# A decoder trunk on one NeuronCore: operand blocks transposed by DMA instead of by TensorE

## The chip, the cores and the metric

The kernel runs on one core of one Trainium2 chip. The metric is the device time of one execution in microseconds (us), given as the median of several runs. One more execution was recorded by the hardware profiler, and all rows below come from it.

Engines: TensorE (PE; its weight loads are PEld), VectorE (DVE), ScalarE (ACT), GpSimd (POOL) and SyncE (SP, whose queue issues nearly all DMAs). Each works through its instructions in order and waits for the others by semaphores.

## The reference, cut to what matters

Two layers of a decoder trunk on x of 256 x 1024 float32. The FFN and the norms are left out here but for their calls.

```python
x = x + 0.5 * swiglu(rms_norm(x, ffn1_norm), ffn1_w_gu, ffn1_w_down)
h = rms_norm(x, mix_norm)
u, va, q, k, v, qi, ki, wi, g_a, g_b = split(h @ w_in)   # 512 each for u..qi; 64, 8, 1024, 1024
y_a = (gelu(u) * (tril(w_s) @ layer_norm(gelu(va)) + b_s)) @ w_pa
q, k, qi, ki = rope(q), rope(k), rope(qi), rope(ki)
score = sum_h(relu(qi_h @ ki.T) * wi_h)          # causal; the 64 best keys of each row are kept
y_b = softmax(q @ k.T / 8 over the kept keys) @ v @ w_pb     # 8 heads of 64
x = x + (sigmoid(g_a + b) * y_a + sigmoid(g_b + b) * y_b) @ w_out
x = x + 0.5 * swiglu(rms_norm(x, ffn2_norm), ffn2_w_gu, ffn2_w_down)
```

## The kernel before

The 256 rows are two blocks t = 0, 1 of 128 rows, one row to a partition. Every large product is taken in three passes (`mm3`, L238): both operands are split into a rounded part hi and a remainder lo, and hi x hi, hi x lo and lo x hi are added up in PSUM. The stationary operand has to lie with the contracted dimension on the partitions, so whatever was computed row by row is transposed in 128 x 128 blocks first.

**Weights** come as a list of tiles of 128 x 1024 words (424 columns twice for the gates) in the order of use. `issue_dma` (L101) loads one into one of four raw buffers from the SP queue; `issue_split` (L121) makes hi on ScalarE (L136) and lo on VectorE (L137), in two halves, into one of six buffers of split tiles. `done(n)` (L150) is called when TensorE has used tile n for the last time; it issues the split of the tile six further on, and this issues the load of the tile four beyond that one. On the SP queue the order is that of the program, written out by hand; on the other engines a planner orders the instructions from the program's order and its own estimates of when each is ready.

**A layer** is an FFN, the mixer, and a second FFN. In the FFN each block h of 128 x 256 goes through `h_send` (L300): ScalarE copies the 32-bit words into two planes of 16-bit halves (L303), the SP queue issues one DMA that transposes the planes in 128 x 128 blocks (L305), and `h_join` (L308) puts the halves together again on VectorE (L311) and splits them into hi and lo (L290, L291).

**The mixer** first runs eleven projections (list `PROJ`, L873; loop at L671): the first gate part with ki and wi, then qi (c = 5), k (3), q (2), v (4), va (1), u (0), and four more gate parts. Each is a `proj` (L260) for t = 0 and for t = 1, 24 matmuls each, with four weight tiles. The result is evacuated by `evac` (L638). Work that needs TensorE later is put into `hooks` and runs inside a following `proj`, after its third weight tile (L271). For q, k and qi, `evac` rotates the block on VectorE (`rope`, L433) and hooks `headsT` (L457), which makes four TensorE transposes into a PSUM bank (L460) and one evacuation on ScalarE (L461) into qT, kT or qiT. `index_scores` (L477), hooked in the fourth and fifth projection, multiplies qiT and kiT, takes the relu on ScalarE (L491), adds up the heads on VectorE (L501, L503) and runs eight rounds of MAX8 and MATCH_REPLACE8 (L512, L513). `attn_scores` (L522), hooked in the seventh and ninth, multiplies qT and kT (L530), takes the maxima on VectorE (L543) and the exponentials on ScalarE (L547). `spatial` (L625) leaves the gated values gm in place of u; `operandT` (L603), hooked in the tenth and eleventh projection, transposes them on TensorE (L607) and splits them (`split`, L597). `attn_out` (L553) is spread in steps between the matmuls of the last two projections.

Then come the two output projections (`outproj`, L691), which are multiplied by the gates and merged into gg (`merge`, L710), and the product with w_out (`wout`, L726). For that gg is transposed on TensorE and split by `xT_half` (L225, transposes on L211), two halves for each t; those of t = 1 in `m1` (L740), called in the middle of the second `wout`.

Of the kernel before, what the change touches and what calls it, by code (L numbers as in the profile page):

```python
# [10 lines left out]
F32 = mybir.dt.float32  # L11
F32R = mybir.dt.float32r
I32 = mybir.dt.int32
U16 = mybir.dt.uint16
# [6 lines left out]
P = 128  # L21
# [25 lines left out]
def hybrid_kernel(ctx: ExitStack, tc: tile.TileContext, a: dict, out: bass.AP):  # L47
# [11 lines left out]
    def bank(tag, bufs):  # L59
        return psum.tile([P, 512], F32, name=tag, tag=tag, bufs=bufs)  # L60
# [111 lines left out]
    def rsqrt(dst, v, scale, eng, plus=None):  # L172
# [12 lines left out]
        for i in range(3):  # L185
# [4 lines left out]
            else:  # L190
                eng.tensor_scalar(u, y, y, h, op0=OP.mult, op1=OP.mult)
                eng.tensor_scalar(to, u, 1.5, y, op0=OP.subtract, op1=OP.mult)

    rstd = [None, None]
    xhi, xlo = [None, None], [None, None]
# [12 lines left out]
    def xT_trans(t, h, src, tr=None):  # L208
        tr = tr or bank("tr", 2)
        for i in range(4):  # L210
            PE.transpose(tr[:, i * P:(i + 1) * P], src[:, h * 512 + i * P:h * 512 + (i + 1) * P], ident)  # L211
        return tr
# [11 lines left out]

    def xT_half(t, h, src, gain):  # L225

        tr = xT_trans(t, h, src)
        if gain is None:
            v = tr.rearrange("p (k q) -> p k q", k=4)
            S.copy(xhi[t][:, 4 * h:4 * h + 4, :], v)  # L230
            V.tensor_tensor(xlo[t][:, 4 * h:4 * h + 4, :], v,
                            xhi[t][:, 4 * h:4 * h + 4, :].bitcast(F32), OP.subtract)
            return
        for part in range(2):
            for k in range(4 * h, 4 * h + 4):
                xT_split(t, k, tr, gain, (part,))
# [39 lines left out]
    def ffn_sub(l, f, gain_next, first=None, ahead=None, final=None):  # L276
# [22 lines left out]

        def h_send(h):  # L300

            pl = work.tile([P, 2, 256], U16, name="planes", tag="sc")
            S.copy(pl, h.bitcast(U16).rearrange("p (c b) -> p b c", b=2))  # L303
            plT = work.tile([P, 4, P], U16, name="planesT", tag="wk")
            nc.sync.dma_start_transpose(plT, pl.rearrange("p b c -> p (b c)"))  # L305
            return plT

        def h_join(j, t, plT):  # L308

            w = work.tile([P, 2, P], F32, name="words", tag="rp2")  # L310
            V.tensor_copy(w.bitcast(U16).rearrange("p k (q b) -> p b k q", b=2),  # L311
                          plT.rearrange("p (b k) q -> p b k q", b=2))
            h_split(j, t, w)
# [15 lines left out]
        for j in range(FC):  # L329
            if j == 0 and first is not None:  # L330
                p0, p1 = first()
                h0 = h_evac(j, 0, p0)
                h1 = h_evac(j, 1, p1)
            else:
                if j == FC - 3 and ahead is not None:
                    ahead()
                tiles = take(4)
                h0 = h_evac(j, 0, proj(tiles, 0, 512, False))
                if j < FC - 1:
                    s0 = h_send(h0)  # L340
                h1 = h_evac(j, 1, proj(tiles, 1, 512, True))
            if j == 0:
                if first is not None:
                    s0 = h_send(h0)
                s1 = h_send(h1)
                hooks.append(lambda s0=s0: h_join(0, 0, s0))
                hooks.append(lambda s1=s1: h_join(0, 1, s1))
                continue
            if j < FC - 1:
                s1 = h_send(h1)  # L350
                dt = take(2)
                down(j - 1, 0, dt, False)
                down(j - 1, 1, dt, True)
                h_join(j, 0, s0)
                hooks.append(lambda j=j, s1=s1: h_join(j, 1, s1))
            else:
                h_trans(j, 0, h0)
# [63 lines left out]
    def mixer(l, loads):  # L421
# [34 lines left out]

        def headsT(dst, src, t):  # L457
            tr = bank("tr", 2)
            for i in range(4):
                PE.transpose(tr[:, i * P:(i + 1) * P], src[:, i * P:(i + 1) * P], ident)  # L460
            S.copy(dst[:, :, t * P:(t + 1) * P], tr.rearrange("p (k q) -> p k q", k=4))  # L461

# [139 lines left out]

        def operandT(key, src, t):  # L603
            new_operand(key, t)
            tr = bank("tr", 2)
            for i in range(4):
                PE.transpose(tr[:, i * P:(i + 1) * P], src[:, i * P:(i + 1) * P], ident)  # L607
            split(key, t, tr)

# [12 lines left out]

        gm = [None, None]

# [13 lines left out]
        def evac(kind, c, t, ps, bias):  # L638
# [9 lines left out]
            if c in (2, 3, 5):  # L648
                dst = {2: qT, 3: kT, 5: qiT}[c]
                r = work.tile([P, 512], F32, name="roped", tag="roped", bufs=3)  # L650
                rope(r, ps, t, NH)
                hooks.append(lambda: headsT(dst, r, t))
            elif c == 4:
# [12 lines left out]
            6: [lambda: attn_scores(0)],  # L666
            8: [lambda: attn_scores(1)],
            9: [lambda: operandT("gm", gm[0], 0)],
            10: [lambda: operandT("gm", gm[1], 1)],
        }  # L670
# [51 lines left out]
        xT_half(0, 1, gg[:, 0, :], None)  # L722
        merge(1, 1, True)
        acc = [[bank("dn", 4) for _ in range(2)] for _ in range(2)]

# [14 lines left out]
        def m1():  # L740
            new_xT(1)
            xT_half(1, 0, gg[:, 1, :], None)
            xT_half(1, 1, gg[:, 1, :], None)
        wout(0, 1, range(4), ta, False, mid=m1)
        wout(1, 0, range(4), ta, False)
        wout(1, 1, range(4), ta, True)
# [186 lines left out]
```

## Time and profile before

| | us |
|---|---|
| median of 3 runs | 1102.29 (1101.81 to 1102.33) |
| the profiled execution | 1101.6 |
| its span, first to last instruction | 1099.9 |
| TensorE busy | 1089.0 |
| VectorE busy | 763.4 |
| ScalarE busy | 651.5 |

Busy is the time in which an engine had an instruction under way; register, branch and semaphore instructions and the issue of DMAs don't count. Matmuls are pipelined: the duration of one is longer than the step from one to the next. The profiler's view of who waited for whom takes the idle time in front of an instruction and names what ended it.

### The profile page before, as it was taken

The numbers are of one execution on the slowest core, as the hardware profiler recorded it, in microseconds if no ns is written. First come the engines' busy times: TensorE is split into PE (matmuls) and PEld (weight loads), VectorE is DVE, ScalarE is ACT, GpSimd is POOL, SyncE is SP. The second block draws the span as 40 slices with busy tenths as digits, with TensorE's granted clock in tenths as the row PEclk, the third lists the DMA queues.
The fourth block names the chain that finished last, engine by engine and source line by source line (L and its number), as shares of the span: only waits on it lengthen the run. The fifth ranks groups of instructions, "written<-read, shape, count | busy, mean of one in ns | idle before, by whom it ended". The sixth has DMA issues, their size and how long they took to land.

```text
span 1099.9 us, 15283 instructions
## 1 busy us (share of the span) xinstructions
PE 1089.0 (99%) x5158; PEld 910.3 (83%) x5158; DVE 763.4 (69%) x1568; ACT 651.5 (59%) x1305; POOL 37.3 (3%) x99
## 2 busy tenths in 40 slices
PE   9999999999999999999999999999999999999997
PEld 7788888888988888888888888888889888888885
DVE  7666656889957676666676666678999567666655
ACT  7665556555765665565675565564566547655553
POOL 0000000100000100000010000010000001000001
PEclk9999999999999999999999999999999999999998
DMA  8866675644655575665665666756446464766661
GB/s 296 235 215 202 231 249 168 220 153 134 183 182 166 168 237 187 230 211 194 208 204 181 236 210 218 249 170 211 133 146 205 157 195 141 233 213 211 217 221 66
DMA packets 103358, 216.78 MB, mean 197 GB/s; under 512 B 50544, under 2 KB 51952, under 8 KB 103280
## 3 DMA queue, kind: packets, MB, share of 16 engines
q1 hardware_dynamic: 102848, 215.27, 60.1%
q8 instruction: 40, 0.66, 0.2%
q10 hardware_dynamic: 432, 0.55, 0.2%
q14 instruction: 38, 0.31, 0.1%
HBM read 204.25 MB, written 1.05 MB: 187 GB/s over the span
## 4 chain that ended last, share of the span: by engine, by line
PE 96%; DMA 1%; DVE 1%; ACT 1%; issue 0%; ACTq 0%; SPq 0%
PE acc L240 62%; PE dn L240 29%; PE tr L211 1%; PE dn L581 1%; DMA x<-in_x_dram 1%; PE dn L530 1%; PE dn L486 1%; PE tr L571 0%; PE tr L460 0%; DMA raw<-in_gu_dram 0%; DVE lo L137 0%; DMA xt<-in_xt_dram 0%; PE dn L628 0%; ACT hi L136 0%; ACT junk L200 0%; DVE rs_y L189 0%
## 5 line engine op out<-in xcount | busy, mean ns | idle before, releaser
L137 DVE TENSOR_TENSOR lo<-raw,hi 128x512 fp32r<-128x512 f32 (+1 forms) x768 | 489.1, 677 | 148.8 <-ACT hi L136 147.3
L136 ACT CAST hi<-raw 128x512 fp32r<-128x512 f32 (+1 forms) x768 | 430.1, 611 | 133.5 <-DMA raw<-in_gu_dram 62.1
L240 PE MATMUL acc<-hi,xhi 128*128 128x512 f32 (+1 forms) x1040 | 402.9, 388 | 0.1
L240 PE MATMUL acc<-hi,xlo 128*128 128x512 f32 (+1 forms) x1040 | 400.3, 385 | 0.0
L240 PE MATMUL acc<-lo,xhi 128*128 128x512 f32 (+1 forms) x1040 | 399.8, 385 | 0.0
L240 PEld LDWEIGHTS acc<-hi,xhi 128*128 128x128 f32 x1040 | 195.2, 188 | 37.8 <-issue 1.3
L240 PEld LDWEIGHTS acc<-hi,xlo 128*128 128x128 f32 x1040 | 195.3, 188 | 35.8 <-issue 0.7
L240 PEld LDWEIGHTS acc<-lo,xhi 128*128 128x128 f32 x1040 | 195.4, 188 | 35.7 <-DVE lo L137 0.6
L240 PE MATMUL dn<-hi,hh 128*128 128x512 f32 x348 | 136.8, 393 | 0.3 <-ACT hh L290 0.3
L240 PE MATMUL dn<-hi,hl 128*128 128x512 f32 x348 | 135.6, 390 | 0.0
L240 PE MATMUL dn<-lo,hh 128*128 128x512 f32 x348 | 135.5, 389 | 0.0
L290 ACT CAST hh<-words 128x256 fp32r<-128x256 f32 x80 | 32.4, 406 | 97.5 <-DVE words L311 97.5
L282 ACT ACTIVATE sg<-acc,rstd 128x256 f32<-128x256 f32 x86 | 40.7, 473 | 66.6 <-PE acc L240 66.4
L240 PEld LDWEIGHTS dn<-hi,hh 128*128 128x128 f32 x348 | 65.4, 188 | 13.8 <-ACT hh L290 0.7
L240 PEld LDWEIGHTS dn<-hi,hl 128*128 128x128 f32 x348 | 65.3, 188 | 13.8
L240 PEld LDWEIGHTS dn<-lo,hh 128*128 128x128 f32 x348 | 65.4, 188 | 13.1
L311 DVE COPY words<-planesT 128x512 uint16<-128x512 uint16 x80 | 36.7, 460 | 53.5 <-DMA planesT<-planes 53.5
L284 DVE SCALAR_TENSOR_TENSOR h<-acc,rstd,sg 128x256 f32<-128x256 f32 x86 | 41.4, 481 | 39.2 <-ACT sg L282 38.8
L303 ACT COPY planes<-h 128x512 uint16<-128x512 uint16 x80 | 49.3, 618 | 20.7 <-DVE h L284 19.9
L291 DVE TENSOR_TENSOR hl<-words,hh 128x256 fp32r<-128x256 f32 x80 | 33.7, 422 | 17.2 <-ACT hh L290 17.0
L200 ACT ACTIVATE junk<-x 128x1024 bf16<-128x1024 f32 x13 | 13.8, 1058 | 26.4 <-DVE x L400 21.3
L220 ACT ACTIVATE xhi<-tr,gains 128x128 fp32r<-128x128 f32 x80 | 22.3, 376 | 6.5 <-PE tr L211 6.5
(145 smaller groups left out, 719.9 us busy)
## 6 DMA issues: line engine op xcount, KB each, us to landing
raw<-in_gu_dram SPq DMA_DIRECT2D x175, 512.0 KB, 4.5
raw<-in_dn_dram SPq DMA_DIRECT2D x88, 512.0 KB, 6.0
raw<-in_win_dram SPq DMA_DIRECT2D x48, 512.0 KB, 4.2
raw<-in_wg_dram SPq DMA_DIRECT2D x40, 424.0 KB, 3.9
raw<-in_wo_dram SPq DMA_DIRECT2D x16, 512.0 KB, 4.4
raw<-in_pa_dram SPq DMA_DIRECT2D x8, 512.0 KB, 5.3
raw<-in_pb_dram SPq DMA_DIRECT2D x8, 512.0 KB, 3.9
bias<-in_bg_dram SPq DMA_DIRECT2D x10, 212.0 KB, 5.4
```

What stands on the lines that cost most here:

```text
L136: S.copy(hi[:, c], r[:, c])
L137: V.tensor_tensor(lo[:, c], r[:, c], hi[:, c].bitcast(F32), OP.subtract)
L200: S.activation(junk, X[t], AF.Square, accum_out=ss)
L211: PE.transpose(tr[:, i * P:(i + 1) * P], src[:, h * 512 + i * P:h * 512 + (i + 1) * P], ident)
L220: S.activation(xhi[t][:, k, :], v, AF.Copy, scale=g)
L240: PE.matmul(dst, a1, b1, start=start and n == 0, stop=stop and n == 2)
L282: S.activation(sg, ps[:, :256], AF.Silu, scale=rstd[t])
L284: V.scalar_tensor_tensor(h, ps[:, 256:], rstd[t], sg, op0=OP.mult, op1=OP.mult)
L290: S.copy(hh, v)
L291: V.tensor_tensor(hl, v, hh.bitcast(F32), OP.subtract)
L303: S.copy(pl, h.bitcast(U16).rearrange("p (c b) -> p b c", b=2))
L311: V.tensor_copy(w.bitcast(U16).rearrange("p k (q b) -> p b k q", b=2), plT.rearrange("p (b k) q -> p b k q", b=2))
```

## The change

`h_send` becomes three helpers: `planes` (ScalarE copies the words into two planes of half words), `turn` (the DMA transpose from the SP queue) and `join` (the halves into words again, on an engine that is given). The FFN calls them with the sizes, tags and engines as before. New users are, in each layer: the rotated q, k and qi of both t (`planes` right behind `rope`; `turn` in the hook that held the TensorE transposes; `join` on ScalarE one hook later, straight into qT, kT or qiT); the gated values of both t (`gm_send`, hooked in the ninth and tenth projection, and `gm_join` one projection later); and the second half of the merged gates of t = 1 (`turn` right behind the last `merge`, `join` in a new `m2` in the middle of the third `wout`). Each of these is 128 x 512 words, so 128 x 1024 half words. The other three halves of gg, all of x, and ki are transposed on TensorE as before.

```diff
--- before.py
+++ after.py
@@ -191,6 +191,24 @@
                 eng.tensor_scalar(u, y, y, h, op0=OP.mult, op1=OP.mult)
                 eng.tensor_scalar(to, u, 1.5, y, op0=OP.subtract, op1=OP.mult)
 
+
+    def planes(src, tag):
+
+        pl = work.tile([P, 2, src.shape[-1]], U16, name="planes", tag=tag)
+        S.copy(pl, src.bitcast(U16).rearrange("p (c b) -> p b c", b=2))
+        return pl
+
+    def turn(pl, tag, bufs=None):
+        k = pl.shape[-1] // P
+        plT = work.tile([P, 2, k, P], U16, name="planesT", tag=tag, bufs=bufs)
+        nc.sync.dma_start_transpose(plT.rearrange("p b k q -> p (b k) q"), pl.rearrange("p b c -> p (b c)"))
+        return plT
+
+    def join(dst, plT, eng):
+
+        (S.copy if eng is S else eng.tensor_copy)(
+            dst.bitcast(U16).rearrange("p k (q b) -> p b k q", b=2), plT)
+
     rstd = [None, None]
     xhi, xlo = [None, None], [None, None]
 
@@ -222,9 +240,9 @@
             V.scalar_tensor_tensor(xlo[t][:, k, :], v, g, xhi[t][:, k, :].bitcast(F32),
                                    op0=OP.mult, op1=OP.subtract)
 
-    def xT_half(t, h, src, gain):
-
-        tr = xT_trans(t, h, src)
+    def xT_half(t, h, src, gain, turned=False):
+
+        tr = src if turned else xT_trans(t, h, src)
         if gain is None:
             v = tr.rearrange("p (k q) -> p k q", k=4)
             S.copy(xhi[t][:, 4 * h:4 * h + 4, :], v)
@@ -297,19 +315,9 @@
                 PE.transpose(tr[:, i * P:(i + 1) * P], h[:, i * P:(i + 1) * P], ident)
             h_split(j, t, tr[:, :256].rearrange("p (k q) -> p k q", k=2))
 
-        def h_send(h):
-
-            pl = work.tile([P, 2, 256], U16, name="planes", tag="sc")
-            S.copy(pl, h.bitcast(U16).rearrange("p (c b) -> p b c", b=2))
-            plT = work.tile([P, 4, P], U16, name="planesT", tag="wk")
-            nc.sync.dma_start_transpose(plT, pl.rearrange("p b c -> p (b c)"))
-            return plT
-
         def h_join(j, t, plT):
-
             w = work.tile([P, 2, P], F32, name="words", tag="rp2")
-            V.tensor_copy(w.bitcast(U16).rearrange("p k (q b) -> p b k q", b=2),
-                          plT.rearrange("p (b k) q -> p b k q", b=2))
+            join(w, plT, V)
             h_split(j, t, w)
 
         def down(j, t, tiles, last):
@@ -337,17 +345,17 @@
                 tiles = take(4)
                 h0 = h_evac(j, 0, proj(tiles, 0, 512, False))
                 if j < FC - 1:
-                    s0 = h_send(h0)
+                    s0 = turn(planes(h0, "sc"), "wk")
                 h1 = h_evac(j, 1, proj(tiles, 1, 512, True))
             if j == 0:
                 if first is not None:
-                    s0 = h_send(h0)
-                s1 = h_send(h1)
+                    s0 = turn(planes(h0, "sc"), "wk")
+                s1 = turn(planes(h1, "sc"), "wk")
                 hooks.append(lambda s0=s0: h_join(0, 0, s0))
                 hooks.append(lambda s1=s1: h_join(0, 1, s1))
                 continue
             if j < FC - 1:
-                s1 = h_send(h1)
+                s1 = turn(planes(h1, "sc"), "wk")
                 dt = take(2)
                 down(j - 1, 0, dt, False)
                 down(j - 1, 1, dt, True)
@@ -454,11 +462,9 @@
                 V.tensor_tensor(dst, t1[:, None, :w].to_broadcast([P, copies, w]),
                                 t2[:, None, :w].to_broadcast([P, copies, w]), OP.add)
 
-        def headsT(dst, src, t):
-            tr = bank("tr", 2)
-            for i in range(4):
-                PE.transpose(tr[:, i * P:(i + 1) * P], src[:, i * P:(i + 1) * P], ident)
-            S.copy(dst[:, :, t * P:(t + 1) * P], tr.rearrange("p (k q) -> p k q", k=4))
+        def headsT(dst, pl, t):
+            plT = turn(pl, "plT")
+            hooks.append(lambda: join(dst[:, :, t * P:(t + 1) * P], plT, S))
 
         def kiTrans(src, t):
             tr = bank("tr", 2)
@@ -600,12 +606,14 @@
             S.copy(dhi, v)
             V.tensor_tensor(dlo, v, dhi.bitcast(F32), OP.subtract)
 
-        def operandT(key, src, t):
-            new_operand(key, t)
-            tr = bank("tr", 2)
-            for i in range(4):
-                PE.transpose(tr[:, i * P:(i + 1) * P], src[:, i * P:(i + 1) * P], ident)
-            split(key, t, tr)
+        def gm_send(t):
+            gmT[t] = turn(planes(gm[t], "ge"), "plT")
+
+        def gm_join(t):
+            new_operand("gm", t)
+            w = work.tile([P, 4, P], F32, name="words", tag="rp2")
+            join(w, gmT[t], S)
+            split("gm", t, w.rearrange("p k q -> p (k q)"))
 
         def layer_norm(t, ge):
             st = small.tile([P, 6], F32, name="bst", tag="bst")
@@ -620,7 +628,7 @@
                 vn[0], vn[1] = both[:, 0, :], both[:, 1, :]
             V.scalar_tensor_tensor(vn[t], ge, r, lnb, op0=OP.mult, op1=OP.add)
 
-        gm = [None, None]
+        gm, gmT = [None, None], [None, None]
 
         def spatial(t):
             ps = bank("dn", 4)
@@ -649,7 +657,8 @@
                 dst = {2: qT, 3: kT, 5: qiT}[c]
                 r = work.tile([P, 512], F32, name="roped", tag="roped", bufs=3)
                 rope(r, ps, t, NH)
-                hooks.append(lambda: headsT(dst, r, t))
+                pl = planes(r, "ge")
+                hooks.append(lambda: headsT(dst, pl, t))
             elif c == 4:
                 S.activation(vv[:, t, :], ps, AF.Copy, scale=rstd[t])
             elif c == 0:
@@ -664,9 +673,9 @@
             3: [lambda: index_scores(0)],
             4: [lambda: index_scores(1)],
             6: [lambda: attn_scores(0)],
-            8: [lambda: attn_scores(1)],
-            9: [lambda: operandT("gm", gm[0], 0)],
-            10: [lambda: operandT("gm", gm[1], 1)],
+            8: [lambda: attn_scores(1), lambda: gm_send(0)],
+            9: [lambda: gm_join(0), lambda: gm_send(1)],
+            10: [lambda: gm_join(1)],
         }
         for i, (kind, c) in enumerate(PROJ):
             hooks.extend(after.get(i, []))
@@ -721,6 +730,7 @@
         xT_half(0, 0, gg[:, 0, :], None)
         xT_half(0, 1, gg[:, 0, :], None)
         merge(1, 1, True)
+        g1T = turn(planes(gg[:, 1, 512:1024], "ge"), "b2", 4)
         acc = [[bank("dn", 4) for _ in range(2)] for _ in range(2)]
 
         def wout(t, n2, ks, tiles, rel, mid=None):
@@ -740,9 +750,13 @@
         def m1():
             new_xT(1)
             xT_half(1, 0, gg[:, 1, :], None)
-            xT_half(1, 1, gg[:, 1, :], None)
+
+        def m2():
+            w = work.tile([P, 4, P], F32, name="words", tag="b2", bufs=4)
+            join(w, g1T, S)
+            xT_half(1, 1, w.rearrange("p k q -> p (k q)"), None, True)
         wout(0, 1, range(4), ta, False, mid=m1)
-        wout(1, 0, range(4), ta, False)
+        wout(1, 0, range(4), ta, False, mid=m2)
         wout(1, 1, range(4), ta, True)
         tb = take(4)
         wout(0, 0, range(4, 8), tb, False)
```

## Rows read from the trace of the kernel before

**Rows 1.** The page: busy us by engine; the chain that ended last.

```profile
PE 1089.0 (99%) x5158; PEld 910.3 (83%) x5158; DVE 763.4 (69%) x1568; ACT 651.5 (59%) x1305; POOL 37.3 (3%) x99
...
PE 96%; DMA 1%; DVE 1%; ACT 1%; issue 0%; ACTq 0%; SPq 0%
```

**Rows 2.** TensorE's waits, last of three: waiting line, releaser: us, times, longest.

```profile
PE dn L240 <- ACT hh L290: 0.3, 1, 0.3
```

**Rows 3.** Groups by line and shape, TensorE: busy us, mean ns, idle before.

```profile
L460 PE MATMUL tr<-ident,roped 128*128 128x128 f32 x48 | 7.2, 271 | 0.0
...
L211 PE MATMUL tr<-ident,gg 128*128 128x128 f32 x32 | 4.1, 272 | 0.0
...
L607 PE MATMUL tr<-ident,uu 128*128 128x128 f32 x16 | 2.5, 280 | 0.0
```

**Rows 4.** Timeline of TensorE around one group: start us, duration us, instruction.

```profile
208.84 0.39 PE L240 MATMUL acc<-hi,xlo 128*128 128x512 f32 x1
209.07 0.60 PE L460 MATMUL tr<-ident,roped 128*128 128x128 f32 x4
...
209.74 0.40 PE L240 MATMUL acc<-lo,xhi 128*128 128x512 f32 x1
```

**Rows 5.** Groups by line and shape, ScalarE.

```profile
L303 ACT COPY planes<-h 128x512 uint16<-128x512 uint16 x80 | 49.3, 618 | 20.7 <-DVE h L284 19.9 <-DMA fgain<-in_fgain_dram 0.6 <-DVE lo L137 0.3
...
L200 ACT ACTIVATE junk<-x 128x1024 bf16<-128x1024 f32 x13 | 13.8, 1058 | 26.4 <-DVE x L400 21.3 <-DVE x L823 4.5
...
L461 ACT COPY qT<-tr 128x512 f32<-128x512 f32 x4 | 2.3, 585 | 6.8 <-PE tr L460 6.8
```

**Rows 6.** Line 305, the DMA transposes: duration ns min/median/max on the queue; landing.

```profile
L305 SPq DMA_TRANSPOSE planesT<-planes x80: 1189/1197/2396, 25.6 to 1068.5; - x80
...
DMA to landing us min/median/max: 2.3/2.3/7.4
```

**Rows 7.** Waits of the SP queue.

```profile
SPq L112 <- DVE lo L137: 346.8, 202, 10.1
```

**Rows 8.** Stretches: length, then busy PE, PEld, DVE, ACT, POOL; clock, DMA share, GB/s.

```profile
232.00:243.00 11.00, 11.00 (x60) 8.84 (x59) 10.81 (x33) 6.49 (x13) 0.68 (x1) 1.00 0.35 111
243.00:265.00 22.00, 22.00 (x105) 18.04 (x105) 21.36 (x67) 13.39 (x23) 1.67 (x3) 1.00 0.48 148
```

**Rows 9.** Timeline of VectorE; in brackets, idle time before and what ended it.

```profile
229.20 0.29 DVE L501 TENSOR_SCALAR sc<-rr,wi 128x128 f32<-128x128 f32 x1 [2.48 <-ACT rr L491]
...
243.25 0.35 DVE L501 TENSOR_SCALAR sc<-rr,wi 128x256 f32<-128x256 f32 x1
...
270.70 0.69 DVE L543 TENSOR_REDUCE mx<-satt 128x4 f32<-128x512 f32 x1
...
275.09 1.11 DVE L137 TENSOR_TENSOR lo<-raw,hi 128x424 fp32r<-128x424 f32 x2
```

**Rows 10.** Timeline of ScalarE.

```profile
228.57 1.09 ACT L491 ACTIVATE rr<-dn 128x512 f32<-128x512 f32 x2 [0.50 <-PE dn L486]
...
271.42 0.40 ACT L547 ACTIVATE pr<-satt,mx 128x128 f32<-128x128 f32 x1 [2.21 <-DVE mx L543]
...
274.52 1.87 ACT L136 CAST hi<-raw 128x424 fp32r<-128x424 f32 x4
```

**Rows 11.** Timeline of TensorE at the third weight tile of the eighth projection.

```profile
275.68 0.35 PE L240 MATMUL acc<-hi,xhi 128*128 128x424 f32 x1
275.87 0.36 PE L240 MATMUL acc<-lo,xhi 128*128 128x424 f32 x1
```

**Rows 12.** Timeline of the SP queue, three places.

```profile
223.49 0.33 SPq L112 DMA_DIRECT2D raw<-in_win_dram  x1
...
241.44 0.33 SPq L112 DMA_DIRECT2D raw<-in_win_dram  x1
...
348.33 1.53 SPq L112 DMA_DIRECT2D raw<-in_gu_dram  x2
```

**Rows 13.** Timeline of ScalarE in the product with w_out.

```profile
354.25 4.27 ACT L136 CAST hi<-raw 128x512 fp32r<-128x512 f32 x8 [4.17 <-PE dn L240]
```

## The prediction

> **What bounds the kernel now.** I read the page first: TensorE is busy for 99% of the span, and 96% of the chain that ended last is TensorE work [rows 1]. A busy TensorE can still stand and wait, so next comes the view of who waited for whom, on TensorE: it has three rows, two of them from the kernel's first 7 us, and the last is 0.3 us [rows 2]. So TensorE practically never waits, and an instruction taken from its stream is worth its own time, as long as the other engines still deliver in time when TensorE comes earlier. That condition is the question here, so the other views look at the stage where the change lies, the projections of the mixer: how full VectorE is there, and how late each operand is.
>
> **What is removed from TensorE.** The groups by shape give 48 transposes on L460, 16 on L607 and 32 on L211 of gg [rows 3]. The first two disappear, and of the last a quarter (t = 1, second half): 48 + 16 + 8 = 72 transposes in 18 groups of four, nine groups per layer. Their mean of 272 ns is a latency, not what the stream pays. The timeline shows that [rows 4]: from the last matmul before a group to the second one after it 209.74 - 208.84 = 0.90 us pass, where two plain steps take 2 x 0.227 = 0.45 (208.84 to 209.07 is one). A group costs 0.45 us: four steps of about 0.09 to 0.11 and a slow first matmul behind it. 18 x 0.45 = 8.0 us on the path, 4.0 per layer (2.7 by the six groups of qi, k and q, 0.9 by gm, 0.4 by gg). This is the ceiling.
>
> **What is added, by engine.** *ScalarE:* `planes` on 512 words is a copy of 1024 half words; the 512-element one takes 0.618 us and a 1024-element activation 1.058 [rows 5], so about 1.05. `join` in the other direction is likewise 1.05 (it writes with a stride of two where the known copy reads with one; between 0.6 and 2.1 as bounds, I take 1.05, the row of the same size). The twelve evacuations of L461 at 0.585 go [rows 5]. Twelve times (2.1 - 0.6) plus six times 2.1 is 31 us on an engine that is busy 652 of 1100 us [rows 1]; it is free work only where nothing stands behind it. *Sync queue:* 18 more transposes, each twice as wide as the 80 that exist. Those hold the queue for 1.2 us and land 2.3 us after issue, at worst 7.4 [rows 6]. Twice the blocks: between 1.2 and 2.4 on the queue and between 2.3 and 4.6 to landing; I take 2.4 and 3.5 (the wait for the last byte is not doubled). Behind a transpose on this queue stand the weight loads. The loads themselves mostly wait there for VectorE to free a raw buffer, 346.8 us in 202 waits [rows 7], so a transpose largely fills time in which the queue stands anyway; I cost that at nothing, and where the cover is gone the next weight tile comes up to 2.4 us late. *VectorE:* no instruction is added; its subtractions for gm and gg read SBUF in place of PSUM, with as many elements, which I cost at nothing. The renamed FFN helpers issue what they issued before.
>
> **Where the time may be lost again.** While topk runs, VectorE is busy 10.81 of 11 and 21.36 of 22 us [rows 8]. Its saturated stretch begins at 229.20, when the relu of the first index scores releases it, and runs almost without a hole to the maxima of the first attention scores, the first of which starts at 270.70 and ends at 271.39 [rows 9]. ScalarE, in order, stands for 2.21 us before the exponentials until that maximum is there, does eight of them, and only then, at 274.52, the conversion of the third weight tile of the next projection [rows 10]; VectorE's subtraction of it follows at 275.09, two halves in 1.11 [rows 9], so the first half is ready at about 275.65. TensorE begins that tile at 275.68 and needs the subtracted half one step later, at 275.87 [rows 11]. The slack is 0.2 us. TensorE will come to this place 2.7 us earlier, VectorE only by the amount A by which its stretch ends earlier, so TensorE stalls 2.7 - 0.2 - A = 2.5 - A in each layer.
>
> A is at most what TensorE has gained when it does the first index scores: four groups (qi twice, k twice) x 0.45 = 1.8. The relu of these scores, now at 228.57 [rows 10], is ready at 226.8. But `join` of k's first block is due on ScalarE just then: its transpose stands behind the load at 223.49 [rows 12], which is some 1.0 earlier then, issues at about 222.8, lands at 226.2 and is joined until 227.3. That holds the relu back by 0.5, and A = 1.3. The stall is 2.5 - 1.3 = 1.2 per layer, 2.4 in all. Bounds: 0.7 per layer with A = 1.8, and no bound but the transposes' lateness on the other side (rivals).
>
> At the end of the mixer the transpose of the merged gates stands behind the two loads that begin at 348.33 and end at 349.86 [rows 12]. It lands at 353.4, and join and split of that half (1.05 + 0.6) hold ScalarE until 355.05; the conversions of the next weight tiles began at 354.25 [rows 13], so they come 0.8 later. I cost that at 0.2 per layer: the bounds are 0, if TensorE is as far from needing them as that, and 0.8, if it waits for them already, and no wait of that stage stands among TensorE's [rows 2]. gm's joins have a whole projection between sending and use: nothing, and if a probability tile's copy stands behind one, up to 1.
>
> Sum: 8.0 - 2.4 - 0.4 = 5.2 us gained. The profiled execution took 1101.6 us (span 1099.9); it becomes 1096.4. The median of the runs is 0.7 above that execution, so 1102.29 - 5.2 = 1097.1.
>
> **A rule that speaks against the change.** In the trace four transposes of TensorE cost 0.45 us of its stream [rows 4], and a DMA transpose of four blocks lands 2.3 us after issue [rows 6], outside that stream. The Trainium skill (VectorE: DVE Perf Modes, The three transpose paths, with its Rules for kernel authors) says to transpose 128 x 128 on TensorE when a PSUM destination will do, and gives 1309 ns for one block by DMA. As an estimate by that page, eight blocks take 10.5 us; the row's 2.3 us for four contradicts so long a time, and the measurement decides. What late transposes would do here is the fourth rival.
>
> **The rivals.**
> 1. *The full gain.* If the conversion of that third weight tile is put ahead of the exponentials in ScalarE's order, the tie is gone: 8.0 - 0.2 gives 1094.5. For it: TensorE frees that tile's buffer 2.7 us earlier, before the exponentials can start. Against: the order in the trace has it behind them although ScalarE stood idle for 2.21 us [rows 10]. Chance 0.22.
> 2. *ScalarE too full.* If planes and joins make conversions 1 to 1.5 us late inside VectorE's full stretch, VectorE stands in front of them and A falls to 0: stall 2.5 per layer, 8.0 - 5.0 - 0.4 = 2.6, giving 1099.7. For it: VectorE has no room there to wait in [rows 8]. Against: in its first 11 us ScalarE has 6.49 us of work [rows 8]; one planes and two joins for two evacuations make it 6.49 + 3.15 - 1.17 = 8.5, and that fits. Chance 0.17.
> 3. *Slower: join of q in front of the second relus.* The transpose of q's first block stands behind the load at 241.44, which waits for VectorE [rows 7, 12]. Shifted by 1.3 it issues at 240.5 and lands at 244.0 to 245.1. If its join is ordered in front of the four relus of the second index scores, these come at 245.0 to 246.2, and VectorE, which used the first at 243.25 [rows 9], wants it at 241.95 and stands until 245.6 to 246.8, some 3.6 to 4.9. Then A = -2.3 to -3.6, the stall is 4.8 to 6.1 per layer, and 8.0 - 9.6 - 0.4 = -2.0 to -4.6: 1104.3 to 1106.9. It loses from A below -1.5 (stall over 4.0). Against: the relus need TensorE alone, which is early, and the join needs a late load. Chance 0.10.
> 4. *Transposes as late as the worst row*, 7.4 us to landing [rows 6]: q's join then holds ScalarE until about 249, the conversions behind it are some 3 us late, A = -1.5, and the gain is 8.0 - 8.0 - 0.4: 1102.7. Chance 0.05.
>
> **How the numbers follow.** The forecast (stall 0.7 to 2 per layer, 1095.5 to 1098.9) has 0.46. What a measurement can tell from no change is 0.2%, 2.2 us: the line for faster is 1100.1. Faster takes the forecast, the full gain and half of rival 2: 0.46 + 0.22 + 0.08 = 0.76. Within 0.2% (1100.1 to 1104.5) lie the other half of rival 2, rival 4 and the mild end of rival 3: 0.15. Slower gets the rest of rival 3: 0.09. The range reaches from the ceiling, 1102.3 - 8.0 less a little, 1093.8, to 1102.8, which leaves out rival 3 and some 0.04 below.
>
> **What would show it.** TensorE has 5086 instead of 5158 matmuls and no tr rows of roped and uu; the Sync queue has 98 transposes, the new ones at about 2.4 us. ScalarE has 18 copies planes and 18 words or head copies of about 1.05. TensorE's waits show a new row on the weights (hi or lo, L136/L137) of 1 to 1.5 us near the first gate projection behind the attention scores, in both layers. Were there no such row, rival 1 is right; were it over 4 us, with VectorE's relu wait (sc on rr) long, rival 3. The forecast is wrong as a whole if a stall appears in the FFN stages, which the change leaves alone, or if a group turns out cheaper than 0.45.

## The result and the profile after

| | us |
|---|---|
| before, median of 6 runs on the same chip | 1102.07 (1101.24 to 1104.13) |
| after, median of 6 runs | 1108.97 (1108.07 to 1109.76) |
| ratio after to before | 1.0059, 95% interval 1.0049 to 1.0070 |
| profiled execution of after, and its span | 1109.76, 1108.0 |

The change costs 6.9 us; the prediction said 5.2 us gained, with a range that ended at 1102.8. The profiled execution is the slowest of the six. Five lines of the page and of TensorE's waits show the kind of failure: the busy times by engine, the chain that ended last, and who kept TensorE waiting (waiting line, releaser: us in all, times, longest).

```profile
PE 1088.4 (98%) x5086; PEld 905.9 (82%) x5086; DVE 761.9 (69%) x1568; ACT 680.0 (61%) x1329; POOL 37.5 (3%) x99
...
PE 78%; issue 11%; DVE 5%; DMA 3%; ACT 3%; POOL 0%; SPq 0%; ACTq 0%; POOLq 0%
...
PE dn L587 <- ACT pT L579: 3.1, 3, 2.3
...
PE acc L258 <- DVE rs_y L183: 1.3, 2, 0.7
PE acc L258 <- ACT vv L663: 1.3, 1, 1.3
```

The 72 transposes are gone (5086 matmuls in place of 5158 [rows 1]) and ScalarE has 28.5 us more, near the 31 that were foreseen. But the chain is no longer TensorE alone: its share fell from 96% [rows 1] to 78%, and TensorE now waits for ScalarE and VectorE within the mixer, which it never did before [rows 2].

Where this happens can be read off TensorE's position. The table gives, for some weight tiles (counted from 0 in the order of use), how much later than in the trace of before TensorE starts on the tile. The projections of layer 1 use the tiles 66 to 109 (four each), those of layer 2 the tiles 258 to 301. The first row is what each execution lost before the mixer, where the renamed helpers do the same work as before: 0.2 and 0.9 with the whole change in it, 2.1 with the least, so it is not put down to the change.

| tile | what comes there | after | gated values back on TensorE (e1) | transposes left out (e3) | both repairs (e7) |
|---|---|---|---|---|---|
| 66 | layer 1, first projection | 0.9 | 1.1 | 2.1 | 0.2 |
| 85 | heads transposed | -1.9 | -1.7 | -0.7 | -2.7 |
| 93 | end of VectorE's full stretch | 0.2 | 0.2 | -0.6 | -2.5 |
| 103 | before the gated values' joins | 0.2 | 0.2 | -0.6 | -2.3 |
| 106 | behind the first of them | 3.5 | 0.2 | -1.0 | -2.7 |
| 130 | layer 1, mixer done | 3.0 | -0.3 | -1.9 | -3.6 |
| 277 | layer 2, heads transposed | 0.1 | -3.1 | -4.7 | -6.4 |
| 285 | end of VectorE's full stretch | 3.1 | -0.7 | -4.5 | -6.2 |
| 302 | behind the gated values | 8.5 | -0.7 | -5.4 | -7.0 |
| 383 | last tile | 8.0 | -1.1 | -5.8 | -7.5 |

In after each layer gains 2.8 us while the heads leave TensorE, as reckoned (2.7), and loses it again at two places: 2.1 and 3.0 us inside VectorE's full stretch, and 3.3 and 5.4 us at the gated values (net of what the groups gain that leave there). The FFN stages add nothing (3.0 at tile 130 and at 258).

**The gated values.** Timeline of ScalarE in after, layer 1, with the idle time in front of an instruction and what ended it in brackets; then the SP queue.

```profile
292.01 1.36 ACT L209 COPY words<-planesT 128x1024 uint16<-128x1024 uint16 x1 [4.38 <-DMA planesT<-planes]
293.38 1.28 ACT L553 ACT_TABLE_LOAD   x1
294.68 0.51 ACT L553 ACTIVATE pr<-satt,mx 128x256 f32<-128x256 f32 x1
...
298.63 1.87 ACT L136 CAST hi<-raw 128x424 fp32r<-128x424 f32 x4
...
308.46 1.36 ACT L209 COPY words<-planesT 128x1024 uint16<-128x1024 uint16 x1 [3.77 <-DMA planesT<-planes]
```

```profile
280.17 5.62 SPq L112 DMA_DIRECT2D raw<-in_wg_dram  x4
286.54 0.33 SPq L169 DMA_DIRECT2D bias<-in_bg_dram  x1
286.92 1.51 SPq L204 DMA_TRANSPOSE planesT<-planes  x1
...
302.70 1.23 SPq L204 DMA_TRANSPOSE planesT<-planes  x1
```

The planes were ready at 281.3 and 282.8, but the turns stand behind four weight loads and a bias load in the queue's written order, or a whole projection later, and go out at 286.92 and 302.70. ScalarE's order has the join in front of the table load, the eight exponentials and four weight conversions; ScalarE stands for 4.38 us with all of them behind it. TensorE's own waits there are 0.73 and 0.58 us in layer 1 (at 299.21 and 300.25) and 0.39, 0.58, 0.46 and 2.31 us in layer 2 (844.26 to 860.70); in each layer the granted clock falls behind them, which takes some 1.7 us more (an estimate, worked out in the last section). Together that is 3.0 of the 3.3 us and all of the 5.4.

**The heads.** Timeline of ScalarE around both sets of relus in after.

```profile
226.75 1.35 ACT L209 COPY kT<-planesT 128x1024 uint16<-128x1024 uint16 x1 [1.49 <-DMA planesT<-planes]
227.96 1.04 ACT L198 COPY planes<-roped 128x1024 uint16<-128x1024 uint16 x1
228.90 1.09 ACT L497 ACTIVATE rr<-dn 128x512 f32<-128x512 f32 x2
...
240.60 1.37 ACT L209 COPY qT<-planesT 128x1024 uint16<-128x1024 uint16 x1 [2.36 <-DMA planesT<-planes]
241.83 1.04 ACT L198 COPY planes<-roped 128x1024 uint16<-128x1024 uint16 x1
242.76 2.06 ACT L497 ACTIVATE rr<-dn 128x512 f32<-128x512 f32 x4
```

In front of each set of relus stand a join, its wait and a copy into planes. With 0.9 for the start taken off, the first relus come 0.6 earlier than before (228.57 [rows 10]), not 1.8, and the second ones at 241.86, no earlier than before (241.67). The second relus and the second maximum (`mx`) of before:

```profile
241.67 2.07 ACT L491 ACTIVATE rr<-dn 128x512 f32<-128x512 f32 x4 [0.47 <-PE dn L486]
```

```profile
271.36 0.69 DVE L543 TENSOR_REDUCE mx<-satt 128x4 f32<-128x512 f32 x1
```

VectorE's scores wait for the relus in after (the last lines are the maxima of layer 1 and the first of layer 2):

```profile
229.54 0.29 DVE L507 TENSOR_SCALAR sc<-rr,wi 128x128 f32<-128x128 f32 x1 [1.10 <-ACT rr L497]
243.39 0.35 DVE L507 TENSOR_SCALAR sc<-rr,wi 128x256 f32<-128x256 f32 x1 [0.58 <-ACT rr L497]
270.86 0.68 DVE L549 TENSOR_REDUCE mx<-satt 128x4 f32<-128x512 f32 x1
...
272.25 0.68 DVE L549 TENSOR_REDUCE mx<-satt 128x4 f32<-128x512 f32 x1
...
816.26 0.68 DVE L549 TENSOR_REDUCE mx<-satt 128x4 f32<-128x512 f32 x1
```

In layer 2 half of the loss stands at another wait. Of the 3.0 us, 1.5 are lost between the tiles 277 and 278, where TensorE stands 1.34 us at 793.56 (the row vv above). It needs the PSUM bank that ScalarE frees when it evacuates the values v of t = 0, and ScalarE comes to that only behind the join of the queries' second half:

```profile
791.62 1.34 ACT L209 COPY qT<-planesT 128x1024 uint16<-128x1024 uint16 x1 [1.40 <-DMA planesT<-planes]
792.83 0.68 ACT L663 ACTIVATE vv<-acc,rstd 128x512 f32<-128x512 f32 x1
```

In e1 below this wait is 0.25 us and layer 2 still loses 2.4 there, so VectorE's stretch would have taken most of the 1.5 anyway; that is argued from the two traces.

### The profile page after: what moved, and what is told of

Its sections match the earlier page's. It is cut to its first block, busy times and chain, and to the rows that moved or that the text cites. A ratio compares the mean times of both kernels' runs of the same rounds, so it can differ in the third digit from the quotient of the medians.

```text
span 1108.0 us, 15207 instructions
## 1 busy us (share of the span) xinstructions
PE 1088.4 (98%) x5086; PEld 905.9 (82%) x5086; DVE 761.9 (69%) x1568; ACT 680.0 (61%) x1329; POOL 37.5 (3%) x99
## 3 DMA queue, kind: packets, MB, share of 16 engines
HBM read 204.25 MB, written 1.05 MB: 185 GB/s over the span
## 4 chain that ended last, share of the span: by engine, by line
PE 78%; issue 11%; DVE 5%; DMA 3%; ACT 3%; POOL 0%; SPq 0%; ACTq 0%; POOLq 0%
PE acc L258 46%; PE dn L258 29%; DVE lo L137 2%; DMA planesT<-planes 2%; PE dn L802 1%; ACT hi L136 1%; DMA bias<-in_bg_dram 1%; PE tr L229 1%; ACT pr L553 1%; DVE wk L519 1%; DVE m L518 1%; PE dn L587 0%; DMA xt<-in_xt_dram 0%; POOL wk L514 0%; PE dn L536 0%
```

## The experiments

All ratios are to the kernel before in runs on the same chip (its medians there: 1102.48, 1102.41 and 1102.47).

**e1, the gated values back on TensorE.** The heads and the quarter of the merged gates stay on the DMA.

```diff
-            8: [lambda: attn_scores(1), lambda: gm_send(0)],
-            9: [lambda: gm_join(0), lambda: gm_send(1)],
-            10: [lambda: gm_join(1)],
+            8: [lambda: attn_scores(1)],
+            9: [lambda: operandT("gm", gm[0], 0)],
+            10: [lambda: operandT("gm", gm[1], 1)],
```

> The changed kernel with the gated values (gm) transposed on TensorE again; heads and merged gates by DMA. Theory A (ScalarE stands in order in front of a join whose transpose lands 5 to 7 us after issue, with the exponentials and weight conversions behind it): in the trace TensorE loses 3.3 us at gm's joins in layer 1 and 5.4 in layer 2, net of what its two fewer groups give. Without them 1109.0 - 8.7 = 1100.3. Theory B (it is the added ScalarE work that costs, wherever it lies): gm is 4 of 18 joins, so 4/18 of the loss of 6.9 + 8.0 = 14.9 goes, 3.3, and 1.8 of TensorE's gain with it: about 1107.5. Theory C (weight loads are late behind the transposes on the Sync queue): as B, by the number of transposes.

Measured 1100.99, ratio 0.9986 (0.9976 to 0.9995). The gated values account for 8.0 us (1108.97 less 1100.99; 8.4 with each taken against before on its own chip); the place where they lose is the right one, and theories B and C are some 6.5 us off. The heads' loss stays (table).

**e2, only the gated values by DMA.** The other half: `headsT` and the merged gates as before.

> Only gm by DMA; heads and merged gates on TensorE as before. Theory A: before plus 8.7, 1110.8, with ScalarE idle in front of each gm join for 3 to 5 us. Theory B and C: 1102.1 - 1.8 + 3.3 = 1103.6.

Measured 1112.29, ratio 1.0085 (1.0067 to 1.0102). Alone this part costs 9.8 us, 1.1 more than was foreseen. ScalarE stands 18.7 us in front of the four joins, up to 6.5 at a time.

**e3, the ceiling.** The 72 transposes are left out and nothing takes their place: the blocks go on unturned.

```diff
-            tr = bank("tr", 2)
-            for i in range(4):
-                PE.transpose(tr[:, i * P:(i + 1) * P], src[:, i * P:(i + 1) * P], ident)
-            S.copy(dst[:, :, t * P:(t + 1) * P], tr.rearrange("p (k q) -> p k q", k=4))
+            S.copy(dst[:, :, t * P:(t + 1) * P], src.rearrange("p (k q) -> p k q", k=4))
```

> The 72 TensorE transposes are left out, and nothing is put in their place: the blocks are copied or split untransposed, so this part of the computation is missing. It measures the term 18 groups x 0.45 us. If the groups cost what the prediction says and nothing else binds: 1102.1 - 8.0 = 1094.1. If the prediction's tie to VectorE's full stretch holds as well (A = 1.8, stall 0.7 per layer): 1095.5, with waits of TensorE on hi or lo near the eighth projection. If a group costs only its 128-column share, 0.25 us: 1097.6.

Measured 1094.97, ratio 0.9933 (0.9918 to 0.9948): 7.5 us, and 7.9 between the traces (-5.8 at the last tile less 2.1 at the start). The 0.45 us a group [rows 4] are confirmed. TensorE waits nowhere in the mixer, so the tie that the prediction saw in VectorE's stretch costs nothing when no join stands in front of the relus.

**e4, all joins on GpSimd.**

```diff
-            hooks.append(lambda: join(dst[:, :, t * P:(t + 1) * P], plT, S))
+            hooks.append(lambda: join(dst[:, :, t * P:(t + 1) * P], plT, G))
-            join(w, gmT[t], S)
+            join(w, gmT[t], G)
-            join(w, g1T, S)
+            join(w, g1T, G)
```

> All 18 new joins on GpSimd in place of ScalarE; planes stay on ScalarE, transposes as in the change. Theory A: GpSimd waits for the landings instead, with nothing urgent behind it: ScalarE's waits on planesT vanish, and the time falls to 1095 to 1098 (the stall at VectorE's full stretch stays). Theory B: the same direction, 24 of 43 us of added ScalarE work gone: 1109.0 - 0.57 x 14.9 = 1100.5. Theory C: transposes and loads stand as they did, 1109.

Measured 1100.96, ratio 0.9987 (0.9978 to 0.9997). That is theory B's figure and not theory A's 1095 to 1098; what parts the two is e5, with the same work. ScalarE waits for no turn any more and the loss at the gated values is gone, but 3 us per layer are still lost in VectorE's stretch (-2.2 at tile 85, 0.8 at 93). The reason is probably another one. GpSimd, then VectorE, in this kernel:

```profile
240.04 1.61 POOL L209 COPY qT<-planesT 128x1024 uint16<-128x1024 uint16 x1 [4.33 <-DMA planesT<-planes]
243.65 1.69 POOL L209 COPY qT<-planesT 128x1024 uint16<-128x1024 uint16 x1 [2.00 <-DMA planesT<-planes]
```

```profile
240.56 1.58 DVE L137 TENSOR_TENSOR lo<-raw,hi 128x512 fp32r<-128x512 f32 x1
242.33 0.68 DVE L137 TENSOR_TENSOR lo<-raw,hi 128x512 fp32r<-128x512 f32 x1
...
243.65 0.47 DVE L509 SCALAR_TENSOR_TENSOR sc<-rr,wi,sc 128x256 f32<-128x256 f32 x1
244.24 1.31 DVE L509 SCALAR_TENSOR_TENSOR sc<-rr,wi,sc 128x256 f32<-128x256 f32 x1
```

Under each of these two joins one VectorE instruction takes 0.84 or 0.90 us longer than its like (1.31 for 0.47, 1.58 for 0.68), 1.7 us in a stretch that has no room. Under the two joins of the keys, at 227.91 and 230.82, two more take 0.55 and 0.67 longer. Together that is 3.0 us, the size of the loss in layer 1; that it is the cause is argued from these sizes. The Trainium skill (SBUF — State Buffer, SBUF: two separate sides) calls the port pair of the two engines an exclusive lock: of a VectorE operation with two SBUF inputs and a GpSimd one that reads SBUF, the one that starts first blocks the other to its end. The rows above agree: both lengthened instructions end just behind the join (242.14 behind 241.65, 245.55 behind 245.34).

**e5, the gated values' turns sent early.** The same work on every engine; `gm_send` runs behind the loads of the tiles 104 and 105.

```diff
             if last:
                 done(n)
+                if sends and len(sends) > q:
+                    sends[q]()
...
+            sends = [lambda: gm_send(0), lambda: gm_send(1)] if i == 7 else None
-            evac(kind, c, 1, proj(tiles, 1, w, True), bias)
+            evac(kind, c, 1, proj(tiles, 1, w, True, sends=sends), bias)
```

> Same work as in the changed kernel on every engine; only the two turns of the gated values are issued earlier on SP's queue, right behind the loads of the tiles 104 and 105 (about 281.3 and 283.3 us in layer 1, where the planes are ready at 281.3 and 282.8) and no longer at 286.9 and 302.7. Theory A (ScalarE stands in front of a transfer that was sent late, with the exponentials and the weight conversions behind it): with landings of 4.5 to 5.5 us the planes are back by 289, before the exponentials are due at 290; the losses of 3.3 and 5.4 us go, and 1108.97 - 8.7 = 1100.3, or from the run without gm's part 1101.0 - 4 x 0.45 = 1099.2. Theory B (ScalarE has too much work there: 4 x (1.04 + 1.36) = 9.6 us of planes and joins in both layers): the work is the same, so no less than 1107.

Measured 1099.32, ratio 0.9969 (0.9958 to 0.9981), as theory A has it (1099.2 to 1100.3). At the gated values it is not the work on ScalarE, it is the wait. ScalarE in e5:

```profile
285.45 1.36 ACT L209 COPY words<-planesT 128x1024 uint16<-128x1024 uint16 x1 [1.53 <-DMA planesT<-planes]
286.68 1.87 ACT L136 CAST hi<-raw 128x424 fp32r<-128x424 f32 x4
288.46 1.35 ACT L209 COPY words<-planesT 128x1024 uint16<-128x1024 uint16 x1
...
291.20 0.51 ACT L555 ACTIVATE pr<-satt,mx 128x256 f32<-128x256 f32 x1
```

The exponentials begin 3.5 us sooner than in after (291.20 for 294.68; 0.3 of that is the start), although the first turn needs 5.1 us to land here too.

**e6, joins behind the relus.** e1, and in addition the joins of the keys' and queries' first half wait for the relus, by a copy of one word of a relu's result (`relu[0]`) that the join overwrites. The scores' hooks (`index_scores`, `attn_scores`) are put ahead of the other hooks; that part isn't in the lines below.

```diff
+            def late_join():
+                if t == 0 and dst is not qiT:
+                    S.copy(dst[:1, 0, :1], relu[0][:1, :1])
+                join(dst[:, :, t * P:(t + 1) * P], plT, S)
-            hooks.append(lambda: join(dst[:, :, t * P:(t + 1) * P], plT, S))
+            hooks.append(late_join)
```

> Gated values transposed on TensorE as before the change (as in e1_no_gm, 1101.0). Heads by DMA, but the joins of the keys' and queries' first half stand behind the relus of the index scores on ScalarE instead of ahead of them; all else the same. Theory A (the loss of 2.1 to 2.9 us per layer between the tiles 85 and 93 is VectorE's full stretch starting late, because each relu stands behind a join of 1.36 us and the wait in front of it): the relus start some 1.4 us earlier against TensorE's position (about 227.6 and 241.0 in layer 1), and 1.3 to 1.9 us per layer come back: 1097.2 to 1098.4. Theory C (weights arrive late because their loads stand behind the turns on SP's queue) or D (planes and joins as such make ScalarE late with the weight conversions): neither is touched, 1100.5 to 1101.5.

Measured 1096.88, ratio 0.9947 (0.9932 to 0.9962): 4.1 us less than e1 (1100.99) and 0.3 below the hopeful end of theory A. ScalarE in e6:

```profile
226.77 1.05 ACT L198 COPY planes<-roped 128x1024 uint16<-128x1024 uint16 x1 [1.45 <-DVE roped L460]
227.72 1.08 ACT L502 ACTIVATE rr<-dn 128x512 f32<-128x512 f32 x2
...
238.93 1.04 ACT L198 COPY planes<-roped 128x1024 uint16<-128x1024 uint16 x1 [1.88 <-DVE roped L460]
239.88 2.06 ACT L502 ACTIVATE rr<-dn 128x512 f32<-128x512 f32 x4
```

The weight loads stand behind the same turns as in e1 and ScalarE has the same copies, so neither of these (theories C and D) was the cause. The order of the hooks and the wait of the joins were changed together, here and in e7 and e8; no run parts them.

**e7, both repairs.** The whole change with the edits of e5 and e6.

> The two edits above together, nothing of the change undone: gated values' turns early, joins of the keys' and queries' first half behind the relus. Theory A for both: 1099.7 (the mean of 1099.2 and 1100.3) less 2.6 to 3.8 = 1096 to 1097. If only the early turns count: 1099.2 to 1100.3. If neither: 1107 or more.

Measured 1094.58, ratio 0.9929 (0.9912 to 0.9945). It lies 1.4 us below what theory A gave for both. It beats both kernels, before by 7.8 us and after by 14.4 (after was timed on another chip), and gets what e3 gets without any transposing. TensorE waits 2.6 us at the kernel's start and 0.7 after it, and the chain reads as that of before did:

```profile
PE 96%; DMA 1%; DVE 1%; ACT 1%; issue 0%; SPq 0%; ACTq 0%
```

The first and the second maximum of layer 1 in e7:

```profile
268.12 0.68 DVE L557 TENSOR_REDUCE mx<-satt 128x4 f32<-128x512 f32 x1
...
269.51 0.68 DVE L557 TENSOR_REDUCE mx<-satt 128x4 f32<-128x512 f32 x1
```

**e8, which relus decide.** e7 with the queries' join in front of the second relus again (`if t == 0 and dst is kT`).

> As e7_both (1094.6), but the join of the queries' first half is put back ahead of the second relus; the join of the keys' first half stays behind the first relus. Theory A1 (the second relus decide: behind the queries' join with its wait of 2.4 us they come 2.9 us later against TensorE, and VectorE's stretch can end no earlier): the losses of 2.1 and 2.9 us in the two layers come back, 1094.6 + 4 to 5 = 1098.6 to 1099.6. Theory A2 (the first relus decide, from which VectorE is full): 1094.6 to 1095.5. If both share in it: about 1097.

Measured 1096.83, ratio 0.9949 (0.9934 to 0.9964), 2.3 us above e7 and near the 1097 that was put for both sharing in it. So neither decides alone: the join in front of the second relus brings back 0.8 and 0.9 us of the loss in the two layers, out of 2.1 and 3.0 in after. The rest goes with the first relus, and in layer 2 also with the wait for vv.

**e9, the turns on another queue.** The change as it is, with its 18 wide turns issued on ScalarE's DMA queue.

```diff
-        nc.sync.dma_start_transpose(
+        (q or nc.sync).dma_start_transpose(
```

> The changed kernel with its 18 wide turns issued on ScalarE's DMA queue, in the place behind their planes, and none of them on SP's: the weight loads stand behind no turn, the turns behind no load. Theory F (a turn lands late because loads stand ahead of it on its own queue: 4.5 to 6.7 us behind loads, 2.7 without): all land in 2.7 to 3.3 us. Theory D (the DMA engines are shared, whichever queue sends): still 4.3 to 5.8 us where loads are in flight. In time: the turns of the gated values go out at about 281 and 283 us, so the 8.7 us lost behind them go (1100.3); ScalarE holds each of the 18 turns for some 1.2 us more; the joins of the queries come up to 2 us earlier under F. Under F 1098 to 1100, under D 1100 to 1103.

Measured 1153.92, ratio 1.0446 (1.0411 to 1.0482): both figures missed, and theory F is wrong. Issues of single turns with the time to landing, first after (242.89, 235.78 and 847.76 us), then e9 (227.02, 243.76 and 370.40):

```profile
planesT<-planes SPq DMA_TRANSPOSE x1, 2.7
planesT<-planes SPq DMA_TRANSPOSE x1, 4.8
planesT<-planes SPq DMA_TRANSPOSE x1, 6.7
```

```profile
planesT<-planes ACTq DMA_TRANSPOSE x1, 2.7
planesT<-planes ACTq DMA_TRANSPOSE x1, 8.3
planesT<-planes ACTq DMA_TRANSPOSE x1, 11.7
```

The stretches from issue to landing (length, granted clock, busy share of the DMA engines, GB/s) of the first two of each:

```profile
242.90:245.60 2.70, 1.00 0.57 109
235.80:240.60 4.80, 1.00 0.94 213
```

```profile
227.00:229.70 2.70, 1.00 0.43 97
243.80:252.10 8.30, 1.00 1.02 202
```

On either queue a turn lands in 2.7 us where the DMA engines are half idle (busy share 0.57 and 0.43), and later where weight loads keep them busy (0.94 and 1.02). On SP's queue a turn holds the loads behind it back, on ScalarE's the loads go on past it; that this is why it lands later still is argued, not shown. ScalarE, in order, then stands in front of the joins, up to 9.9 us, and TensorE behind it.

## Why the prediction was wrong, point by point

- **The ceiling** (0.45 us a group, 8.0 in all) was right: 7.5 by e3, 7.8 by e7 (each against the median of before on its chip).
- **gm's joins, "nothing", and at most 1: the step that failed most, with 8.7 us of loss.** It was reasoned from TensorE, a whole projection between sending and use. But the instruction that waits is ScalarE's, and ScalarE comes to it where its own order has it, ahead of the exponentials. 4.38 and 3.77 us of waiting in layer 1 made 3.3 us of loss, and 5.4 in layer 2; e5 took it away without removing any work. The two questions that were asked for k and gg (behind what does the turn stand on the queue, what stands behind the join on ScalarE) were not asked for gm. The SP queue of before would have shown it: there too four weight loads go out in a row from 280.00 on, and a bias load at 286.44.
- **The tie in VectorE's stretch: VectorE's late end was foreseen, its A was mis-sized.** The sum took stall = 2.5 - A, A being how much earlier the stretch ends. Taken at the first maximum, less the start (0.9; 3.0 by layer 2), it now ends at 269.96 and 813.26, before at 270.70 [rows 9] and 813.21: A is 0.7 and -0.1 where 1.3 was put. The formula then gives 1.8 and 2.6; 2.1 and 3.0 were lost, in place of 1.2 each. (The order has changed too: the first maximum now stands between the two additions of the mask, `satt`, and no longer behind both. By the second maximum, 272.25 for 271.36 and 817.65 for 813.88, A is 0.0 and -0.8.) Two joins in front of the relus made A so small: that of k, which was allowed 0.5 and took the first relus from 1.8 earlier to 0.6, and that of q, which was rival 3 with a chance of 0.10. Rival 3 had the right mechanism and too high a price (4.8 to 6.1 per layer; e8 shows 0.8 and 0.9 for q alone), since the turn of q went out at 235.78, not at 240.5.
- **The bound on A, 1.8, left out a change of order.** In e7 the first maximum comes at 268.12, less the start's 0.2 at 267.92, and A is 270.70 - 267.92 = 2.8. By the second maximum A is 2.0 (269.51 - 0.2 for 271.36), and the first relus are 1.9 earlier (226.84 - 0.2 = 226.64 for 228.57), so the 1.8 was nearly right; the new order of the maxima gives the other 0.8. So e3 and e7 have no stall, where the forecast's best case still had 0.7 per layer. Rival 1's time, 1094.5, is that of e7, reached for another reason than the one it named: that they agree is luck.
- **The stall showed up at another place** than foretold: at the tiles 86 to 92, whose lo is made inside the stretch, and in layer 2 also at vv, not at tile 96, the third of the gate projection, where nothing was lost.
- **Durations.** `planes` 1.04 (1.05 foreseen). `join` on ScalarE 1.36 (1.05). The queue is mostly held for 1.23 and at most for 1.99 (2.4 was taken, 1.2 the lower bound). Landing was taken as 3.5 between 2.3 and 4.6: it is 2.7 to 6.7. No wide turn of after reached rival 4's 7.4.
- **Turns in front of the loads, "nothing"**: right; e6 and e7 have the same turns of the heads there and lose next to nothing (0.3 in layer 2 of e6).
- **Rival 2** (ScalarE too full, A = 0, 1099.7) describes the heads' loss in size, not in cause: the same copies in another order lose nothing (e6).
- **gg**: 0.2 per layer was charged. The gain of 0.45 arrives in full (3.4 at tile 118, 3.0 at 126 in after).
- **Sums.** By the prediction's own terms (stall 0.7 to 2, gg 0.4 in all) the forecast reaches from 1096.1 to 1098.7, not from 1095.5 to 1098.9; rival 1, with gg at 0.4, is 1094.7; and the change loses from A below -1.3, not -1.5. None of this bears on the outcome.

## What to carry to other kernels

When a step is handed from the engine that bounds the kernel to a DMA and a second engine, ask of every new waiting instruction what is queued behind it there, and where the transfer stands in its queue; the time until the result is needed says nothing as long as the waiter is in order. Send the transfer as soon as its source is ready and let the waiting instruction come last on its engine: here that turned 0.6% lost into 0.7% gained with the same work.

## What was not expected of the hardware

- A transpose of eight blocks lands in 2.7 us with the DMA engines half busy (shares of 0.56 to 0.69 in after), in 3.1 to 6.7 elsewhere on SP's queue (shares of 0.86 and more, once 0.66), and in up to 11.7 on ScalarE's.
- ScalarE's copy of 1024 half words takes 1.04 us when it reads with a stride of two (`planes`) and 1.36 us when it writes with a stride of two (`join`).
- TensorE's clock fell where it had been made to wait. Stretches of after (length, TensorE's busy time and count, granted clock, DMA share, GB/s):

```profile
290.00:300.00 10.00, 8.94 (x49) 1.00 0.39 108
300.00:301.90 1.90, 1.52 (x11) 1.00 0.16 23
301.90:305.30 3.40, 3.27 (x15) 0.51 0.83 219
```

TensorE had stood for some 1.4 us of the 11.9 ahead; then the granted clock was 0.51, the lower of its two levels (1.2 and 2.4 GHz), for 3.4 us: a matmul of 424 columns stepped 0.36 us there (304.50 to 304.86), and 0.19 behind it (306.05 to 306.24). As an estimate, half of the 3.4 us, 1.7, was lost there. The same happens in layer 2 (0.50 from 861.7 to 865.1), but not behind the single wait of 1.34 us at 793.56, where the granted clock stayed at 1.00. In the mixers of before, e1, e5 and e7 it never fell.
